# Hybrid decoder layer: x factor loads spread in time, eight weight buffers in the branches, the partial sum added by an accumulating load, residual rows later

## Chip, cores and metric

The kernel runs on one core of a Trainium2 chip. The metric is the device time in microseconds (us) of one execution. The engines are PE (TensorE; PEld is its weight load), DVE (VectorE), ACT (ScalarE), POOL (GpSimd) and SP (SyncE, here only an issuer of DMAs).

## What is computed

One layer for 544 tokens: 512 of a prompt and 8x4 decode tokens. D = 2048, E = 1024. Cut to what matters here:

```
proj = rmsnorm(x) @ w_in                       # 2048 -> 14336: eight parts of 1024, then gpre, 3 x 2048
conv_out = (cb * conv(cc * ch) * silu(cz)) @ w_conv_out            # 1024 -> 2048
ys = gelu(s5(su) * silu(sz))
ssm_out = (ys @ w_glu_a) * sigmoid(ys @ w_glu_b)                   # 1024 -> 2048, twice
attn_out = (attention(aq, memory) * silu(az)) @ w_attn_out         # 1024 -> 2048
g = sigmoid(gpre)
merged = g[0] * conv_out + g[1] * ssm_out + g[2] * attn_out
y = rmsnorm(x + merged @ w_out) * final_norm_g                     # the layer, then the final norm
```

The outputs also hold the new memory keys and values and the new states. All is fp32.

## The kernel before, in words

**Numbers.** Every fp32 operand of a large product is split into a hi part in fp32r (a copy on ACT) and a lo part (source minus hi, on DVE): `split`, L113 to L115. A product is then three matmuls, hi by hi, hi by lo and lo by hi. Weights come from DRAM as raw tiles of 512 KB, loaded by SP, and each is split on the chip. `ws["mark"]` is the lo tile of the latest weight split; `hold` (L135) is a one-element copy on POOL which reads it, so that what POOL issues after it waits for that split.

**Tokens.** T = 544 tokens are two halves of NH = 272; a large matmul is 128x128 by 128x272.

**Stages, in order of time.** First memory keys and values, then projections by `w_in` with `proj` (L149ff, matmuls in L172 to L178), with the convolution, the S5 layer and the attention running beside them as queued pieces (`tick`, `bg`, `later`). One more projection (L1075) opens the silu and gelu of the S5 branch; from there on `w_in` is used by `winograd` (L1083 to L1131): a 2x2 block scheme with seven products in place of eight, n = 1, 5, 6, 3, 7, 2, 4, each 24 matmuls, over x factors XT[n]. XT[1, 2, 3] lie in the x tiles; XT[5], XT[6] and XT[4] are loaded from DRAM (`xf_d`) into tiles of their own, XT[7] over a part of the x tiles that the projection of L1075 still reads. Three `winograd` columns finish the S5 branch's gate, 24 give the sigmoid gates, which go to DRAM (`gt_d`). Beside them `branch_factors` (L1138) writes the seven factors of each branch to DRAM (`fd`).

**Branches, L1188 to L1296.** `winograd2` (L1212 to L1264) is the same scheme for the branch weights: SP loads four raw weight tiles of 512 columns, then seven products of 24 matmuls each follow. For the sums of two weight tiles DVE uses L1243 to L1251. `load_factors` (L1204) loads a branch's 14 factor tiles on POOL into one of two sets, `fsets`. `gate` (L1266) loads two gate tiles, on SP. There are four columns q per weight matrix. Branch 2 (attention) and branch 0 (convolution): the result times the gate goes to `mg_d` in DRAM, first by a plain store, then by a store that adds (L1285). Branch 1: `w_glu_a` times the gate, then `w_glu_b`, sigmoid, product, and an adding store (L1296). The ring of raw weight tiles has 4 + 2 (`bxr`) members.

**Output, L1301 on.** POOL loads the eight tiles of the sum from `mg_d` (L1308), ACT and DVE split them into `mh`, `ml` (L1310). POOL loads the residual rows of x into `yt` (L1323 to L1325). Then eight column blocks jp of `w_out`: a projection, and `residual`, which transposes the result back, adds it to `yt`, squares and scales; the last block also finishes the norm.

**Order.** Each engine works through its own list in order. SP's list holds the weight loads and the gate loads as they are written; a load waits until its buffer is free, and everything behind it on SP waits with it. POOL's list holds factor loads, stores, sum loads and row loads.

Of the kernel before, what the change touches and what calls it, by code (L numbers as in the profile page):

```python
# [20 lines left out]
T = 544  # L21
# [6 lines left out]
def hybrid_step_kernel(  # L28
# [12 lines left out]
    with ctx:  # L41
# [116 lines left out]
        def flush():  # L158
            while later:
                later.pop(0)()  # L160
# [881 lines left out]
        for n in (5, 6, 4):  # L1042
            for hl in range(2):
                P.dma_start(out=XT[n][hl], in_=xf_d[n][hl])
        brs = ExitStack()
# [31 lines left out]
        for hl in range(2):  # L1077
            P.dma_start(out=XT[7][hl], in_=xf_d[7][hl])
# [109 lines left out]
        frs = ExitStack()  # L1188
        fsets = []
        for i in (1, 0):  # L1190
            pool = frs.enter_context(tc.tile_pool(name=f"fset{i}", bufs=1, side="right", reuse_waits="tile"))
            fsets.insert(0, {n: tuple(pool.tile([128, 4, NH], F32R, name=f"b{hl}{n}_{i}") for hl in "hl")
                             for n in (4, 2, 7, 3, 6, 5, 1)})
        mtp = brs.enter_context(tc.tile_pool(name="mgt", bufs=2, reuse_waits="tile"))
# [4 lines left out]
        bxr = bps.enter_context(tc.tile_pool(name="bxr", bufs=2, reuse_waits="tile"))  # L1199
        pbA = bps.enter_context(tc.tile_pool(name="pbA", bufs=2, space=PSUM, reuse_waits="tile"))  # L1200
        pbB = bps.enter_context(tc.tile_pool(name="pbB", bufs=2, space=PSUM, reuse_waits="tile"))
        rings([bxr] * 2, [bxh])
# [9 lines left out]
        def winograd2(w, col0, F, before=None):  # L1212
# [7 lines left out]
            if before:  # L1220
                before()
# [44 lines left out]
        def gate(br, q):  # L1266
            sg = [sgp.tile([128, 2, T], F32, name="sgate") for _ in range(2)]
            for i in range(2):
                nc.sync.dma_start(out=sg[i], in_=gt_d[br, 2 * q + i])
            return sg  # L1270

        def run(g):
            for _ in g:
                pass

        rate[0] = 1
        for br, w, F, nxt in ((2, w_attn_out[0], fsets[0], 1), (0, w_conv_out[0], fsets[1], 2)):
            for q in range(4):
                o = winograd2(w, q * 512, F, (lambda: run(load_factors(F, fd[0], False))) if (br, q) == (2, 0) else None)
                if not q:  # L1280
                    bg.append(load_factors(fsets[nxt % 2], fd[nxt]))
                sg = gate(br, q)
                for i in range(2):
                    V.tensor_mul(o[i], o[i], sg[i])
                    P.dma_start(out=mg_d[2 * q + i], in_=o[i], **({} if br == 2 else {"accum_op": ALU.add}))  # L1285
            tick(1000)
        for q in range(4):
            o = winograd2(w_glu_a[0], q * 512, fsets[0])
            sg = gate(1, q)
# [3 lines left out]
            for i in range(2):  # L1293
                S.activation(o[i], o[i], AF.Sigmoid)
                V.tensor_mul(o[i], o[i], sg[i])
                P.dma_start(out=mg_d[2 * q + i], in_=o[i], accum_op=ALU.add)  # L1296
        bps.close()
        frs.close()
# [4 lines left out]
        mhp = ctx.enter_context(tc.tile_pool(name="mhp", bufs=1, side="right", reuse_waits="tile"))  # L1303
        mh = [mhp.tile([128, T], F32R, name=f"mh{j}") for j in range(16)]
        ml = [mhp.tile([128, T], F32R, name=f"ml{j}") for j in range(16)]
        for i in range(8):
            t = mtp.tile([128, 2, T], F32, name="mgt")
            P.dma_start(out=t, in_=mg_d[i])  # L1308
            for j in range(2):
                split(mh[2 * i + j], ml[2 * i + j], t[:, j])  # L1310
        brs.close()
# [11 lines left out]
        for i in range(5):  # L1323
            hold(yt[i][:, 0:1])
            load_rows(yt[i], i, P)  # L1325
# [41 lines left out]
        for jp in range(7):  # L1367
# [4 lines left out]
            residual(jp, range(5), oT)  # L1372
# [54 lines left out]
```

## Time and profile before

| | |
|---|---|
| median of 3 runs | 2165.47 us (2164.09 to 2172.06) |
| profiled execution, its own time | 2164.23 us |
| span of the profile | 2161.8 us |
| PE busy | 2068.0 us, 96% |
| DVE, ACT, POOL busy | 1284.9, 809.9, 439.5 us |
| mean granted clock of TensorE | 0.984 |
| moved by DMA | 363.59 MB, mean 168 GB/s |
| the chain that ended last | PE 80%, DMA 7%, DVE 5%, POOL 2%, issue 2%, ACT 1% |

The span is that of the trace; the time of the execution is 2.4 us longer. "Busy" counts what an engine computes; for PE a matmul that runs at half clock is busy twice as long, so a high share can hide lost time. "Granted clock" is the share of full speed that TensorE was allowed: 1.00 is 2.4 GHz, 0.50 is 1.2 GHz. In the chain of waits, one follows back from the last instruction what released each step.

### The profile page before, as it was taken

What the parts mean: (1) busy time and instruction counts of PE and PEld (TensorE: products, weight loads), DVE (VectorE), ACT (ScalarE), POOL (GpSimd) and SP (SyncE); (2) the same over time, 40 slices, a digit from 0 to 9 for tenths busy, and PEclk for the clock granted to TensorE, in tenths of its full rate; (3) what the DMA queues carried; (4) which work ended last, traced back from release to release, by engine and by line L of the source; (5) the groups of instructions that cost most, each with busy time, mean ns of one, the idle gap of its engine ahead of it and who ended that gap; (6) DMA issues with size and microseconds to landing.
All of it is one profiled execution on the core that took longest, in us unless ns stands there. A gap on an engine that the chain in (4) does not pass through costs nothing.

```text
span 2161.8 us, 38757 instructions
## 1 busy us (share of the span) xinstructions
PE 2068.0 (96%) x16122; PEld 2016.1 (93%) x16122; DVE 1284.9 (59%) x1877; ACT 809.9 (37%) x1153; POOL 439.5 (20%) x518
## 2 busy tenths in 40 slices
PE   7999999999999999989999999999999899969996
PEld 5899999999999998879999999999899899969996
DVE  6664367943134743238887877767587686753232
ACT  6622222122122433224555555444444344433232
POOL 1008970054201102110121111000121100021121
PEclk9999999999999999999999999999999999989998
DMA  8747612234344626486677776643697955474223
GB/s 261 224 156 143 126 59 90 89 116 108 99 118 146 182 90 224 173 299 172 198 241 221 212 214 207 181 129 110 217 345 252 293 142 164 144 184 137 88 89 83
DMA packets 341619, 363.59 MB, mean 168 GB/s; under 512 B 62507, under 2 KB 288387, under 8 KB 338661
## 3 DMA queue, kind: packets, MB, share of 16 engines
q1 hardware_dynamic: 263712, 211.19, 33.2%
q0 software_dynamic: 38960, 118.48, 17.7%
q10 hardware_dynamic: 38772, 31.46, 5.0%
q8 instruction: 126, 2.06, 0.4%
q14 instruction: 49, 0.39, 0.1%
HBM read 280.82 MB, written 79.73 MB: 167 GB/s over the span
## 4 chain that ended last, share of the span: by engine, by line
PE 80%; DMA 7%; DVE 5%; POOL 2%; issue 2%; ACT 1%; ACTq 1%; DVEq 0%; SPq 0%; POOLq 0%
PE pA L1103 14%; PE pB L1103 11%; PE mmps L172 11%; PE mmps L178 11%; PE mmps L175 11%; PE pbA L1232 5%; PE pbB L1232 4%; DMA raw<-in_w_glu_b_dram 2%; DVE wlo L115 2%; DMA mgt<-mg_d 1%; PE mmps L324 1%; PE mmps L323 1%; PE mmps L325 1%; DMA raw<-in_w_in_dram 1%; DMA bl<-fd 1%
## 5 line engine op out<-in xcount | busy, mean ns | idle before, releaser
L115 DVE TENSOR_TENSOR wlo<-raw,whi 128x1024 fp32r<-128x1024 f32 x395 | 505.9, 1282 | 462.9 <-ACT whi L114 456.0
L114 ACT ACTIVATE whi<-raw 128x1024 fp32r<-128x1024 f32 x395 | 418.5, 1060 | 836.4 <-PE mmps L175 406.0
L172 PE MATMUL mmps<-xh,whi 128*128 128x272 f32 x1856 | 390.3, 291 | 1.5 <-ACT whi L114 1.3
L175 PE MATMUL mmps<-xl,whi 128*128 128x272 f32 x1856 | 389.6, 289 | 0.0
L178 PE MATMUL mmps<-xh,wlo 128*128 128x272 f32 x1856 | 386.7, 289 | 1.1 <-DVE wlo L115 1.1
L175 PEld LDWEIGHTS mmps<-xl,whi 128*128 128x128 f32 x1856 | 293.7, 188 | 4.3 <-issue 4.1
L172 PEld LDWEIGHTS mmps<-xh,whi 128*128 128x128 f32 x1856 | 290.9, 188 | 6.9 <-issue 4.5
L178 PEld LDWEIGHTS mmps<-xh,wlo 128*128 128x128 f32 x1856 | 290.9, 188 | 5.0 <-issue 2.7
L1232 PE MATMUL pbA<-bh,whi 128*128 128x272 f32 x512 | 149.5, 292 | 6.6 <-DVE bo L1256 5.0
L1232 PE MATMUL pbA<-bl,whi 128*128 128x272 f32 x512 | 149.1, 292 | 1.8 <-DMA bl<-fd 1.8
L1232 PE MATMUL pbA<-bh,wlo 128*128 128x272 f32 x512 | 148.9, 292 | 0.0
L1103 PE MATMUL pB<-xh,whi 128*128 128x272 f32 x432 | 126.2, 292 | 3.1 <-ACT whi L114 3.1
L1103 PE MATMUL pB<-xh,wlo 128*128 128x272 f32 x432 | 125.7, 291 | 0.0
L1232 PE MATMUL pbB<-bh,wlo 128*128 128x272 f32 x384 | 113.8, 296 | 12.0 <-DVE wlo L115 12.0
L1103 PE MATMUL pB<-xl,whi 128*128 128x272 f32 x432 | 125.3, 290 | 0.0
L1103 PE MATMUL pA<-xth,whi 128*128 128x272 f32 x432 | 124.4, 288 | 0.7 <-DVE sgate L1124 0.6
L1103 PE MATMUL pA<-xh,wlo 128*128 128x272 f32 x432 | 124.8, 289 | 0.0
L1103 PE MATMUL pA<-xh,whi 128*128 128x272 f32 x432 | 124.7, 289 | 0.0
L1103 PE MATMUL pA<-xth,wlo 128*128 128x272 f32 x432 | 124.6, 288 | 0.0
L1103 PE MATMUL pA<-xl,whi 128*128 128x272 f32 x432 | 124.4, 288 | 0.0
L1103 PE MATMUL pA<-xtl,whi 128*128 128x272 f32 x432 | 124.1, 287 | 0.0
L172 PE MATMUL mmps<-mh,whi 128*128 128x272 f32 x448 | 93.9, 294 | 21.0 <-ACT mh L114 21.0
(402 smaller groups left out, 4595.2 us busy)
## 6 DMA issues: line engine op xcount, KB each, us to landing
raw<-in_w_in_dram SPq DMA_DIRECT2D x224, 512.0 KB, 3.9
fd<-fs POOLq DMA_DIRECT2D x84, 272.0 KB, 4.0
raw<-in_w_out_dram SPq DMA_DIRECT2D x32, 512.0 KB, 3.4
gt_d<-sgate ACTq DMA_DIRECT2D x24, 544.0 KB, 3.1
sgate<-gt_d SPq DMA_DIRECT2D x24, 544.0 KB, 7.1
mg_d<-bo POOLq DMA_DIRECT2D x24, 544.0 KB, 8.4
bh<-fd POOLq DMA_DIRECT2D x21, 544.0 KB, 7.7
bl<-fd POOLq DMA_DIRECT2D x21, 544.0 KB, 9.0
```

The source lines that it names most:

```text
L114: S.activation(hi, src, AF.Copy)
L115: V.tensor_sub(lo, src, hi.bitcast(F32))
L172: nc.tensor.matmul(ps[m][:, n, :NH], lh, rh(kt, n), start=(kt == 0), stop=False)
L175: nc.tensor.matmul(ps[m][:, n, :NH], lh, rl(kt, n), start=False, stop=False)
L178: nc.tensor.matmul(ps[m][:, n, :NH], ll, rh(kt, n), start=False, stop=(kt == nk - 1))
L323: nc.tensor.matmul(o, lh, hi[:, q, :], start=(kt == 0), stop=False)
L324: nc.tensor.matmul(o, lh, lo[:, q, :], start=False, stop=False)
L325: nc.tensor.matmul(o, ll, hi[:, q, :], start=False, stop=(kt == 15))
L1103: nc.tensor.matmul(ps, a[:, k, :], t[:, k, :], start=new and i == 0, stop=i == 23, skip_group_check=not new)
L1232: nc.tensor.matmul(ps[:, s], a[:, k, s * 128:(s + 1) * 128], t[:, k, :], start=new and i == 0, stop=i == 11, skip_group_check=not new)
```

## The change

1. XT[5] and XT[6] are loaded first, XT[7] after the projection of L1075, and XT[4] after XT[7], behind two holds. Before, XT[4] came ahead of XT[7].
2. `bxr` has four members, so eight raw weight tiles are in the ring. The gates are loaded on POOL, ahead of `winograd2`, in place of SP behind its weight loads. The second factor set is loaded ahead of the first `winograd2`.
3. In branch 1 nothing is stored: the product is the target of an accumulating load of `mg_d`, o[i] += mg_d[i], and each tile is split when a later `tick` takes it from `later`. The split parts go to the factor tiles of set 1, which are free by then, and the last two pairs to new tiles `mhx`, `mlx`. The loads of the sum and their tiles are gone.
4. The residual rows are loaded after the first projection by `w_out`, and `residual` of a block runs one projection later.

```diff
-        for n in (5, 6, 4):
+        def load_xt(n):
             for hl in range(2):
                 P.dma_start(out=XT[n][hl], in_=xf_d[n][hl])
+        load_xt(5)
+        load_xt(6)
...
         ws["st"].close()
-        for hl in range(2):
-            P.dma_start(out=XT[7][hl], in_=xf_d[7][hl])
+        load_xt(7)
+        for t in XT[4]:
+            hold(t[:, 0, 0:1])
+        load_xt(4)
...
-        bxr = bps.enter_context(tc.tile_pool(name="bxr", bufs=2, reuse_waits="tile"))
+        bxr = bps.enter_context(tc.tile_pool(name="bxr", bufs=4, reuse_waits="tile"))
...
-        rings([bxr] * 2, [bxh])
+        rings([bxr] * 4, [bxh])
...
             for i in range(2):
-                nc.sync.dma_start(out=sg[i], in_=gt_d[br, 2 * q + i])
+                P.dma_start(out=sg[i], in_=gt_d[br, 2 * q + i])
...
-                o = winograd2(w, q * 512, F, (lambda: run(load_factors(F, fd[0], False))) if (br, q) == (2, 0) else None)
+                if (br, q) == (2, 0):
+                    for _ in load_factors(F, fd[0], False):
+                        pass
+                sg = gate(br, q)
+                o = winograd2(w, q * 512, F)
                 if not q:
                     bg.append(load_factors(fsets[nxt % 2], fd[nxt]))
-                sg = gate(br, q)
...
+        mh, ml = [], []
+        for pair in fsets[1].values():
+            for t in pair:
+                t = t.rearrange("p k t -> p (k t)")
+                mh.append(t[:, :T])
+                ml.append(t[:, T:])
+
+        def merged(t, k0):
+            for j in range(2):
+                split(mh[k0 + j], ml[k0 + j], t[:, j])
+
         for q in range(4):
+            sg = gate(1, q)
             o = winograd2(w_glu_a[0], q * 512, fsets[0])
-            sg = gate(1, q)
...
-                P.dma_start(out=mg_d[2 * q + i], in_=o[i], accum_op=ALU.add)
+                P.dma_start(out=o[i], in_=mg_d[2 * q + i], accum_op=ALU.add)
+                if (q, i) != (3, 1):
+                    later.append(lambda t=o[i], k0=4 * q + 2 * i: merged(t, k0))
+        frs[0].close()
+        mhx = ctx.enter_context(tc.tile_pool(name="mhx", bufs=2, side="right", reuse_waits="tile"))
...
+        flush()
+        merged(o[1], 14)
...
-        for i in range(8):
-            t = mtp.tile([128, 2, T], F32, name="mgt")
-            P.dma_start(out=t, in_=mg_d[i])
-            for j in range(2):
-                split(mh[2 * i + j], ml[2 * i + j], t[:, j])
...
-        for i in range(5):
-            hold(yt[i][:, 0:1])
-            load_rows(yt[i], i, P)
...
-            residual(jp, range(5), oT)
+            if not jp:
+                for i in range(5):
+                    hold(yt[i][:, 0:1])
+                    load_rows(yt[i], i, P)
+            else:
+                residual(jp - 1, range(5), prev)
+            prev = oT
+        residual(6, range(5), prev)
```

Three places show how the lists of the engines move. The first is SP's list at the third column of `w_glu_b` (raw is a weight tile, sgate a gate tile). Before:

```order
L1217 DMA raw_19623<-in_w_glu_b_dram 128x4x256
L1217 DMA raw_19625<-in_w_glu_b_dram 128x4x256
L1269 DMA sgate_19617<-gt_d_80 128x1088
L1217 DMA raw_19627<-in_w_glu_b_dram 128x4x256
L1269 DMA sgate_19618<-gt_d_80 128x1088
L1217 DMA raw_19629<-in_w_glu_b_dram 128x4x256
```

and now:

```order
L1223 DMA raw_19638<-in_w_glu_b_dram 128x4x256
L1223 DMA raw_19640<-in_w_glu_b_dram 128x4x256
L1223 DMA raw_19642<-in_w_glu_b_dram 128x4x256
L1223 DMA raw_19644<-in_w_glu_b_dram 128x4x256
```

The gates have left SP. They stand now on POOL, between the accumulating loads:

```order
L1312 DMA bo_19646<-mg_d4_89 128x1088
L1273 DMA sgate_19865<-gt_d_80 128x1088
L1312 DMA bo_19647<-mg_d5_90 128x1088
L1273 DMA sgate_19866<-gt_d_80 128x1088
L1312 DMA bo_20108<-mg_d6_91 128x1088
L1312 DMA bo_20109<-mg_d7_92 128x1088
```

The last two rows are the accumulating loads of the last column; no load of the sum follows them.

The second place is ACT's list from the last column of `w_glu_b` into the output projection (whi is the hi part of a weight tile; L1294 and L1310 are the sigmoids). Before:

```order
L114 ACTIVATE whi_20442<-raw_20440 128x1024
L1294 ACTIVATE bo_20085<-bo_20085 128x1088
L114 ACTIVATE whi_20496<-raw_20494 128x1024
L1262 COPY bo_20086<-pbA_20088 128x2x272
L114 ACTIVATE mh0_20321<-mgt_20353 128x544
L114 ACTIVATE mh1_20322<-mgt_20353 128x544
L114 ACTIVATE mh2_20323<-mgt_20359 128x544
L114 ACTIVATE mh3_20324<-mgt_20359 128x544
L1294 ACTIVATE bo_20086<-bo_20086 128x1088
L114 ACTIVATE whi_20550<-raw_20548 128x1024
L114 ACTIVATE mh4_20325<-mgt_20365 128x544
```

and now:

```order
L114 ACTIVATE whi_20378<-raw_20376 128x1024
L1310 ACTIVATE bo_20108<-bo_20108 128x1088
L114 ACTIVATE whi_20432<-raw_20430 128x1024
L1266 COPY bo_20109<-pbA_20111 128x2x272
L1310 ACTIVATE bo_20109<-bo_20109 128x1088
L114 ACTIVATE bh1_1_16548<-bo_20108 128x544
L114 ACTIVATE bl1_1_16549<-bo_20108 128x544
L114 ACTIVATE whi_20486<-raw_20484 128x1024
L114 ACTIVATE mhx_20331<-bo_20109 128x544
L114 ACTIVATE mhx_20333<-bo_20109 128x544
L114 ACTIVATE whi_20540<-raw_20538 128x1024
```

Before, sixteen hi copies of the sum stood among the splits of the first weight tiles; now four do, two ahead of the third weight tile's split and two ahead of the fourth's.

The third place is POOL's list at the x factors (xth5 is the hi tile of XT[5]; xl and xh are where XT[7] goes). Now:

```order
L1045 DMA xth5_9898<-xf5_82 128x2176
L1045 DMA xtl5_9899<-xf5_82 128x2176
L1045 DMA xth6_9896<-xf6_83 128x2176
L1045 DMA xtl6_9897<-xf6_83 128x2176
L1045 DMA xl_139<-xf7_84 128x8x272
L1045 DMA xh_138<-xf7_84 128x8x272
L137 COPY xth4_9894<-wlo_10086 128x1
L137 COPY xtl4_9895<-wlo_10086 128x1
L1045 DMA xth4_9894<-xf4_81 128x2176
L1045 DMA xtl4_9895<-xf4_81 128x2176
```

Before, the two loads of xth4 and xtl4 stood directly behind those of xtl6, ahead of xl and xh, and without holds.

## Rows read from the trace of the kernel before

**Rows 1.** The page, part 1: busy time of each engine, share of the span, instructions.
```profile
PE 2068.0 (96%) x16122; PEld 2016.1 (93%) x16122; DVE 1284.9 (59%) x1877; ACT 809.9 (37%) x1153; POOL 439.5 (20%) x518
```

**Rows 2.** Table by stretches of the span: stretch and its length, busy time and (instructions) of PE, PEld, DVE, ACT, POOL, then granted clock, share of DMA engines busy, GB/s.
```profile
955.00:1005.00 50.00, 38.14 (x265) 36.94 (x264) 34.85 (x38) 20.82 (x29) 0.00 (x0) 0.86 0.91 269
1005.00:1543.00 538.00, 536.92 (x4279) 536.14 (x4278) 416.07 (x440) 270.20 (x380) 56.48 (x108) 1.00 0.60 183
1543.00:1575.00 32.00, 27.82 (x200) 26.53 (x199) 19.57 (x20) 10.80 (x13) 7.42 (x14) 0.95 1.00 344
1575.00:1675.00 100.00, 100.00 (x801) 100.00 (x800) 81.36 (x76) 46.09 (x54) 21.35 (x50) 1.00 0.90 296
1675.00:1740.00 65.00, 56.60 (x421) 56.16 (x420) 44.23 (x41) 23.02 (x27) 12.17 (x23) 0.92 0.89 268
1740.00:1905.00 165.00, 156.40 (x1207) 155.32 (x1207) 122.04 (x113) 74.75 (x86) 6.26 (x8) 0.97 0.49 142
1905.00:1965.00 60.00, 38.98 (x285) 37.30 (x283) 23.96 (x28) 19.35 (x28) 12.88 (x26) 0.86 0.87 236
1965.00:2125.00 160.00, 159.80 (x1281) 159.34 (x1281) 46.96 (x63) 50.66 (x111) 31.31 (x35) 1.00 0.23 77
```

**Rows 3.** PE's timeline, four of the instructions before which it stood idle: start, duration, engine, line, operation, tiles, and in brackets the idle time and what ended it.
```profile
970.12 0.59 PE L1103 MATMUL pB<-xth,whi 128*128 128x272 f32 x1 [8.66 <-ACT whi L114]
...
1698.88 0.39 PE L1232 MATMUL pbB<-bh,wlo 128*128 128x272 f32 x1 [4.04 <-DVE wlo L115]
...
1796.15 0.59 PE L1232 MATMUL pbB<-bh,wlo 128*128 128x272 f32 x1 [3.07 <-DVE wlo L115]
...
1942.15 1.28 PE L172 MATMUL mmps<-mh,whi 128*128 128x272 f32 x4 [16.89 <-ACT mh L114]
```

**Rows 4.** Two stretches at half clock, columns as in rows 2.
```profile
965.82:976.06 10.24, 5.50 (x22) 5.19 (x23) 7.81 (x7) 2.50 (x3) 0.00 (x0) 0.50 1.25 334
...
1795.30:1802.10 6.80, 5.95 (x26) 5.95 (x27) 6.77 (x8) 0.79 (x1) 0.00 (x0) 0.50 0.65 229
```

**Rows 5.** Around the x factors: DVE's timeline, then the packets, MB and share of 16 engines' time of two DMA queues in 950 to 962 (q0 is POOL's, q1 SP's), of q1 in 964 to 975, and the DMA issues at 940.5 (XT[6], lo) and 941.5 (XT[4], lo): transfers, KB each, us from issue to landing.
```profile
967.69 1.22 DVE L1109 TENSOR_TENSOR sum<-raw 128x1024 f32<-128x1024 f32 x1 [1.15 <-DMA raw<-in_w_in_dram]
...
q0 software_dynamic: 475, 3.72, 76.4%
...
q1 hardware_dynamic: 472, 0.24, 9.7%
...
q1 hardware_dynamic: 1924, 0.97, 44.3%
...
xtl<-xf POOLq DMA_DIRECT2D x1, 1088.0 KB, 16.8
...
xtl<-xf POOLq DMA_DIRECT2D x1, 1088.0 KB, 23.0
```

**Rows 6.** A step of the glu: SP's list of issues, a link of the chain of waits (start, us, what), and DVE's wait for the sum of two weight tiles.
```profile
1782.14 0.34 SPq L1269 DMA_DIRECT2D sgate<-gt_d  x1
1786.08 0.37 SPq L1217 DMA_DIRECT2D raw<-in_w_glu_b_dram  x1
...
1780.93 12.68 DMA raw<-in_w_glu_b_dram
...
1793.73 1.22 DVE L1243 TENSOR_TENSOR bsum<-raw 128x1024 f32<-128x1024 f32 x1 [7.68 <-DMA raw<-in_w_glu_b_dram]
```

**Rows 7.** The end of a glu step (timelines of ACT, DVE and POOL): a weight split's hi part, the copy of the last product, a split's lo part, the two adding stores. Then the copies of the sum's split, all 14 on record: least, median and greatest duration in ns, first and last start. Then how long the stores into `mg_d` took from issue to landing in 1700 to 1900.
```profile
1777.78 1.06 ACT L114 ACTIVATE whi<-raw 128x1024 fp32r<-128x1024 f32 x1 [0.46 <-PE pbA L1232]
1778.75 0.59 ACT L1262 COPY bo<-pbA 128x544 f32<-128x544 f32 x1
...
1784.83 1.23 DVE L115 TENSOR_TENSOR wlo<-raw,whi 128x1024 fp32r<-128x1024 f32 x1 [1.59 <-ACT whi L114]
...
1780.06 0.85 POOL L1296 DMA_DIRECT2D mg_d<-bo  x1 [40.94 <-DVE bo L1295]
1782.40 0.85 POOL L1296 DMA_DIRECT2D mg_d<-bo  x1 [1.49 <-DVE bo L1295]
...
L114 ACT ACTIVATE mh<-mgt x14: 641/650/660, 1918.0 to 1957.6; 128x544 fp32r<-128x544 f32 x14
L115 DVE TENSOR_TENSOR ml<-mgt,mh x14: 717/720/727, 1918.7 to 1958.4; 128x544 fp32r<-128x544 f32 x14
...
DMA to landing us min/median/max: 5.6/9.1/10.2
```

**Rows 8.** DMA issues in 1914 to 1941: transfers, KB each, median us to landing; and a link of the chain of waits there.
```profile
mg_d<-bo POOLq DMA_DIRECT2D x2, 544.0 KB, 16.6
mgt<-mg_d POOLq DMA_DIRECT2D x2, 544.0 KB, 18.1
raw<-in_w_out_dram SPq DMA_DIRECT2D x2, 512.0 KB, 19.0
...
1922.95 18.48 DMA mgt<-mg_d
```

**Rows 9.** DMA queues in 1675 to 1726, from the conv branch's last column into the first glu column: packets, MB, share of 16 engines' time; and the issues of conv weights.
```profile
q0 software_dynamic: 2306, 8.91, 59.5%
q1 hardware_dynamic: 5264, 6.88, 40.5%
...
raw<-in_w_conv_out_dram SPq DMA_DIRECT2D x2, 512.0 KB, 11.3
```

More of the change, by code (lines that the diff above doesn't have):

```diff
@@ L1184, in hybrid_step_kernel @@
         xs.close()
-        frs = ExitStack()
+        frs = [ExitStack(), ExitStack()]
+        ctx.callback(frs[1].close)
         fsets = []
         for i in (1, 0):
-            pool = frs.enter_context(tc.tile_pool(name=f"fset{i}", bufs=1, side="right", reuse_waits="tile"))
+            pool = frs[i].enter_context(tc.tile_pool(name=f"fset{i}", bufs=1, side="right", reuse_waits="tile"))
             fsets.insert(0, {n: tuple(pool.tile([128, 4, NH], F32R, name=f"b{hl}{n}_{i}") for hl in "hl")
                              for n in (4, 2, 7, 3, 6, 5, 1)})
-        mtp = brs.enter_context(tc.tile_pool(name="mgt", bufs=2, reuse_waits="tile"))
         bps = ExitStack()
@@ L1210, in load_factors, with winograd2 @@
                 yield
-        def winograd2(w, col0, F, before=None):
+        def winograd2(w, col0, F):
             blk = {}
@@ L1219, in winograd2 @@
             a11, a12, a21, a22 = blk[0, 0], blk[0, 1], blk[1, 0], blk[1, 1]
-            if before:
-                before()
             def product(ps, n, src, new):
@@ L1268, in gate @@
             for i in range(2):
-                nc.sync.dma_start(out=sg[i], in_=gt_d[br, 2 * q + i])
+                P.dma_start(out=sg[i], in_=gt_d[br, 2 * q + i])
             return sg
-        def run(g):
-            for _ in g:
-                pass
         rate[0] = 1
@@ L1295, in hybrid_step_kernel @@
                 V.tensor_mul(o[i], o[i], sg[i])
-                P.dma_start(out=mg_d[2 * q + i], in_=o[i], accum_op=ALU.add)
+                P.dma_start(out=o[i], in_=mg_d[2 * q + i], accum_op=ALU.add)
[3 more added lines that the diff above has]
+        mhx = ctx.enter_context(tc.tile_pool(name="mhx", bufs=2, side="right", reuse_waits="tile"))
+        for j in range(2):
+            mh.append(mhx.tile([128, T], F32R, name="mhx"))
+            ml.append(mhx.tile([128, T], F32R, name="mlx"))
+        flush()
+        merged(o[1], 14)
         bps.close()
-        frs.close()
+        brs.close()
         rings()
         open_std()
-        mhp = ctx.enter_context(tc.tile_pool(name="mhp", bufs=1, side="right", reuse_waits="tile"))
-        mh = [mhp.tile([128, T], F32R, name=f"mh{j}") for j in range(16)]
-        ml = [mhp.tile([128, T], F32R, name=f"ml{j}") for j in range(16)]
-        for i in range(8):
-            t = mtp.tile([128, 2, T], F32, name="mgt")
-            P.dma_start(out=t, in_=mg_d[i])
-            for j in range(2):
-                split(mh[2 * i + j], ml[2 * i + j], t[:, j])
-        brs.close()
         ytp = ctx.enter_context(tc.tile_pool(name="ytp", bufs=1, side="right", reuse_waits="tile"))
```

## The prediction, written before the change was run

> **What bounds the kernel now.** I read the busy line first: PE works for 96% of the span [rows 1]. One matmul group of this kernel is 128x272, and where nothing disturbs it PE starts 801 of them in 100 us, 8.0 per us, at a granted clock of 1.00, the upper of the two levels, 2.4 GHz [rows 2] (the stretch from 1575 to 1675). So a stretch with fewer matmuls than eight per us has lost the difference, whether PE stood still or ran at half clock. The table of stretches gives: 955 to 1005, 265 matmuls in 50 us, 16.9 us lost (**A**, the start of the x factors); 1543 to 1575, 200 in 32 us, 7.0 lost (**B**, the start of the branches); 1675 to 1740, 421 in 65 us, 12.4 lost, and 1740 to 1905, 1207 in 165 us, 14.1 lost (**C**, 26.5 in all); 1905 to 1965, 285 in 60 us, 24.4 lost (**D**, the merged sum). The rest of the middle is full: 4279 in 538 us and 1281 in 160 us [rows 2]. The change touches only A to D: 74.8 us, so even with all of it gone the time would be 2089.
>
> Then PE's own timeline says what each wait was for [rows 3]. In A, PE waits 8.66 us for a hi copy of ACT; in C, 4.04, 3.07 and similar waits for the lo part of a weight split; in D, 16.89 us for the hi copy of the merged sum. After a long wait the granted clock is 0.50 (1.2 GHz) for a while [rows 4]: 5.50 us of matmuls from 965.82 at half clock lose 2.75 us more. A wait thus costs more than its length, and counting matmuls takes that in.
>
> **The sum, part by part**, against the profiled execution (2164.2 us, 1.2 under the median of 2165.5).
>
> *A, x factors.* ACT waits for DVE's sum of two weight blocks, which waits for the fourth weight load: it can run only at 967.69 [rows 5]. Why is that load late? While XT[5], XT[6] and XT[4] load, the weights' queue q1 moves 472 packets in 12 us, as many as the factors' q0 (475), 39 per us each; a factor packet is some 8 KB and a weight packet 0.5 KB, so the weights get 0.24 MB against 3.72. Later, beside XT[7], which has small packets, q1 moves 1924 in 11 us, 175 per us. The last transfer of XT[6] lands at 940.5+16.8 = 957.3, that of XT[4] at 941.5+23.0 = 964.5 [rows 5]. The change puts XT[4] behind XT[7], so the slow 7.2 us leave the weights' path. Between 957.3 and 967.7 q1 moved about 7.2x39+3.2x175 = 840 packets; at 175 per us they take 4.8 us, so the sum can run 5.6 us earlier. Of the 8.66 us wait 3.1 stay. With half of the 2.75 us at half clock I take **7.0**. Lower end 0: another wait (the gelu steps on DVE and ACT stand in the same order) takes the place. Upper end 14: all but the 3.1. The holds in front of XT[4] wait for the last weight split of the projection, which is over before PE leaves that projection, so before XT[7] is in; behind them on POOL stand only the branch factors, and XT[4] belongs to the last product.
>
> *B, branch start.* Two gates (1.1 MB) leave SP for a place behind the 14 factor loads on POOL, and two more weight loads (1.05 MB) come into the two new buffers. DMA is full there, at 344 GB/s [rows 2], so 3.2 us of transfers go and 3.0 come: **0**, ends -3 and +2.
>
> *C, branches and glu.* On SP a gate stood ahead of the third and the fourth weight load of each block column, and a gate waits for DVE's product with the gate before it. At 1782.14 SP issues the second gate, and the fourth weight load only at 1786.08 [rows 6]; with a landing of up to 12.68 us the chain then goes through that load, and DVE's sum of two weight blocks stands idle 7.68 us for it. In this stretch the DMA engines are busy 0.49 of the time [rows 2]: the load is late because it is issued late. With eight buffers and no gate on SP, all four loads of the next product can be issued as this one's splits free the buffers, a whole product (24x7/8 = 21 us) ahead, against that landing of 12.68. What comes new: in three of the four glu steps ACT and DVE get four merge splits, ACT 4x0.65 and DVE 4x0.72 = 2.9 us [rows 7]; DVE has 122.04 busy of 165 us [rows 2], 15.5 of each 21, so 18.4 with them. It fits, but not always in the right place: I leave half of it, 1.5 us three times. Gain 26.5-4.5 = **22**; ends 12 (first rival) and 26. POOL's issue is dearer (0.85 us for a transfer of this size [rows 7], SP's 0.34 [rows 6]) but on no path, since the gate is needed 21 us later.
>
> *D, merged sum.* Before, the last accumulating store must land, then the load of the sum, both beside the residual rows (544x2048 fp32, 4.5 MB): medians 16.6 and 18.1 us [rows 8]. Afterwards one accumulating load stands there, and the rows come one projection later. Let X be the end of the last branch product. In the glu steps X is 1778.7 and POOL issues the two transfers at 1780.06 and 1782.40, X+1.4 and X+3.7 [rows 7]. An accumulating load does not occur in the trace; the nearest row is the accumulating store of the same tile, 5.6 at the least, 9.1 median, 9.3 at this place and 10.2 at the most [rows 7]. I take 9.3. So the first tile lands at X+10.7; two hi copies (1.3) and the weight split behind them on ACT and DVE (1.06, 1.23) end at X+14.3. ACT has the splits of the output projection's first two weight blocks ahead of these copies, the third behind them, the fourth behind the second tile's. Two blocks are 96 matmuls, so PE has 12 us of work from X on, and then waits 2.3. The second tile lands at X+13.0 and is through at X+16.6, due at X+20.3: no wait. Gain 24.4-2.3 = **22**; ends 14 (a landing of 16.6 even without the rows: 7.3 more, and some half clock) and 24.
>
> *Residuals.* The residual of one projection runs beside the next; 5 and 6 come together before the last block, with 10 transposed tiles on four banks. DVE is busy 46.96 us in 160 [rows 2], 6.7 per projection, of which four weight splits are 4.9; the rest, 1.8 us, is what one more residual could cost. I take **-1**, ends 0 and -3. The rows' loads, now from about X+18, slow the second projection's weights to some 19 us [rows 8]; its last block is issued near X+17 and due at X+42, so it hides.
>
> Sum: 7+0+22+22-1 = 50; 2164.2-50 = **2114**. All lower ends together give 2144, all upper ones 2098.
>
> **Rivals.**
> *DMA engines, not the issue order, bound the end of the conv branch* (0.20). For: in 1675 to 1726 the shares of the queues are 59.5% and 40.5%, together all of the 16 engines' time, and a conv weight load takes 11.3 us [rows 9]. The same bytes must pass. Against: 1740 to 1905 at 0.49. Then the 12.4 us of 1675 to 1740 stay, but for the part that I leave anyway: 10 less gain, **2124**. The Trainium skill ("DMA: Bandwidth & Descriptors", Issuing engines are not separate DMA queues) says that loads of all issuing engines run on the same 16 DMA engines, so that another issuer saves only the time to issue. By that rule moving the gates to POOL is worth nothing where these are full, which the rows of 1675 to 1726 bear out, and something where SP stands waiting, as at 1782.
>
> *The first stage gains nothing* (0.10): the weights come earlier but the gelu chain on ACT and DVE holds the split. **2121**.
>
> *Accumulating loads land late* (0.12). A gate's load stands between the two, and ACT works in order: behind the merge copies stand the weight splits. The second load must be through by the seventh product, X+18: 18-3.7-1.3-1.06-1.23 = 10.7 us at most; beyond it, every microsecond is lost three times, and in D from 9.3 on. At 13 us (between 10.2 and 16.6) that is 3x2.3+3.7 = 10.6, with one stretch at half clock (5.95 us of matmuls at 1795.3 [rows 4], 3 us) some 14: **2128**.
>
> *Slower, by the same wait* (0.03): the cost is 4L-41.4 for a landing of L. At L = 22.9 it eats the 50 us, from 25.6 on the kernel is slower by over 0.5%; at 27 us it is 67, **2181**. For: 18.48 us was seen for a load of the sum [rows 8]. Against: that one stood beside the residual rows, which leave the place, and in the glu stretch nothing took over 10.2.
>
> *The change does not do what it says* (0.02): the scheduler's rows show the new order, so only a wait that I don't see could keep all of it.
>
> **How the numbers follow.** My forecast has 0.53. The range, **2097 to 2140**, runs from nearly all upper ends to nearly all lower ones and holds the first three rivals; outside stay the slower case, no change, and combinations, together under 0.2. A measurement of this kernel tells 0.5%, 10.8 us, from no change. Faster 0.93 (forecast and three rivals, less a rest), the same 0.04, slower 0.03.
>
> **What would show it.** By stretches, matmuls lost against eight per us: A about 10, B 7, C under 6, D under 4. XT[4] lands behind XT[7]; no half clock in the glu steps; four weight loads of a product issued without a gap; accumulating loads landing in 9 to 10 us and in the tail no wait over 3 us. It is wrong if the chain still shows weight loads of the branches (first rival), a wait for ACT hi copies in the middle of glu_a products (third), or if in A the sum still runs at 967.

## The result, and the profile after

The changed kernel takes 2107.19 us (median of 4, 2105.97 to 2112.99), before 2165.24 (2164.09 to 2172.06). The ratio is 0.9731, 95% interval [0.9704, 0.9758]: 58 us faster. The same kernel run again later gave 0.9730 [0.9715, 0.9744]. Forecast: 2114 in a range of 2097 to 2140.

The table by stretches of the kernel after, columns as in [rows 2]:

```profile
955.00:1005.00 50.00, 44.33 (x331) 43.89 (x331) 39.05 (x44) 23.62 (x33) 0.00 (x0) 0.93 0.96 282
1537.00:1569.00 32.00, 27.08 (x197) 26.02 (x196) 19.79 (x19) 10.86 (x13) 7.96 (x15) 0.95 1.00 344
1669.00:1734.00 65.00, 64.97 (x519) 64.75 (x518) 53.46 (x50) 28.36 (x34) 15.06 (x28) 1.00 1.05 325
1734.00:1885.00 151.00, 150.56 (x1201) 150.16 (x1201) 128.31 (x124) 80.41 (x96) 8.44 (x12) 1.00 0.46 134
1885.00:1910.00 25.00, 25.00 (x202) 25.00 (x201) 9.54 (x10) 9.36 (x12) 8.12 (x17) 1.00 0.83 212
```

Against eight matmuls per us the first row now loses 8.6 us (before 16.9), the second 7.4 (7.0), the next two 1.0 together (26.5) and the last nothing (24.4 in the row of 1905 to 1965). The end of the conv branch runs at full rate with the DMA engines busy all the time.

Matmul counts of fixed windows compare badly where the stages shift, so from here on I cut at the same work in each kernel: **A** from the first matmul over x factors to the first of the branches, **B** the first branch product column, **C** from the second to the last glu matmul, **D** from there to the end of the first projection by `w_out`. Each row below is such a stretch of the kernel after, A to D:

```profile
960.72:1541.48 580.76, 572.68 (x4538) 571.26 (x4537) 452.55 (x480) 292.10 (x412) 59.71 (x114) 0.99 0.64 194
1541.48:1568.53 27.05, 23.54 (x169) 22.67 (x170) 14.84 (x14) 7.86 (x9) 5.31 (x10) 0.94 1.07 373
1568.53:1885.11 316.58, 316.11 (x2521) 315.49 (x2520) 264.56 (x249) 154.70 (x183) 52.70 (x100) 1.00 0.71 222
1885.11:1909.36 24.25, 24.25 (x196) 24.25 (x194) 9.44 (x10) 8.72 (x12) 7.61 (x16) 1.00 0.83 213
```

and of the kernel before:

```profile
958.28:1547.80 589.52, 574.90 (x4539) 572.73 (x4537) 454.11 (x480) 292.70 (x412) 60.72 (x116) 0.99 0.63 189
1547.80:1574.26 26.46, 23.96 (x169) 22.87 (x169) 14.20 (x14) 7.86 (x9) 3.18 (x6) 0.94 1.08 377
1574.26:1916.29 342.03, 325.03 (x2521) 323.51 (x2520) 254.99 (x237) 148.12 (x171) 42.43 (x89) 0.97 0.69 213
1916.29:1965.86 49.57, 28.35 (x200) 26.45 (x198) 17.34 (x22) 15.94 (x24) 10.23 (x18) 0.83 0.91 242
```

The gain is 8.8 in A, -0.6 in B, 25.4 in C, 25.3 in D. Ahead of A the kernel after is 2.4 us later, behind D 0.1 later: 56.4, the difference of the two spans (2161.8 and 2105.4). The 2.4 us are scatter: nothing is changed there, and a run of the old program with a later part changed reaches A at 960.98 too.

What PE still waits for in A (timeline of PE, idle time in brackets; before: 8.66 [rows 3]):

```profile
968.33 0.39 PE L1109 MATMUL pB<-xth,whi 128*128 128x272 f32 x1 [4.43 <-ACT whi L114]
970.08 0.59 PE L1109 MATMUL pB<-xth,wlo 128*128 128x272 f32 x1 [1.24 <-DVE wlo L115]
```

The accumulating loads at a glu step and at the end (POOL's list), and their least, median and greatest time to landing; the stores of [rows 7] had 5.6, 9.1 and 10.2:

```profile
1760.54 0.87 POOL L1312 DMA_DIRECT2D bo<-mg_d  x1 [37.94 <-DVE bo L1311]
1761.10 0.85 POOL L1273 DMA_DIRECT2D sgate<-gt_d  x1
1762.88 0.86 POOL L1312 DMA_DIRECT2D bo<-mg_d  x1 [0.93 <-DVE bo L1311]
...
1885.93 0.87 POOL L1312 DMA_DIRECT2D bo<-mg_d  x1 [36.84 <-DVE bo L1311]
1889.70 0.87 POOL L1312 DMA_DIRECT2D bo<-mg_d  x1 [2.90 <-DVE bo L1311]
...
DMA to landing us min/median/max: 5.7/6.5/10.0
```

### The profile page after: what moved, and what is told of

It reads as the page before. It is cut to its first block, busy times and chain, and to the rows that moved or that the text cites. A ratio compares the mean times of both kernels' runs of the same rounds, so it can differ in the third digit from the quotient of the medians.

```text
span 2105.4 us, 38714 instructions
## 1 busy us (share of the span) xinstructions
PE 2053.1 (98%) x16122; PEld 2004.0 (95%) x16122; DVE 1283.5 (61%) x1877; ACT 809.0 (38%) x1153; POOL 447.2 (21%) x536
## 4 chain that ended last, share of the span: by engine, by line
PE 79%; issue 5%; DMA 5%; DVE 4%; POOL 3%; ACTq 1%; ACT 1%; POOLq 0%; SPq 0%; DVEq 0%
PE mmps L178 12%; PE mmps L172 12%; PE mmps L175 11%; PE pA L1109 11%; PE pB L1109 9%; PE pbA L1236 8%; PE pbB L1236 6%; DVE wlo L115 1%; DMA bl<-fd 1%; PE mmps L324 1%; PE mmps L323 1%; PE mmps L325 1%; PE aux L717 1%; DMA raw<-in_w_in_dram 1%; POOL pw L567 1%
## 5 line engine op out<-in xcount | busy, mean ns | idle before, releaser
L1236 PE MATMUL pbB<-bl,whi 128*128 128x272 f32 x384 | 110.4, 288 | 1.8 <-DMA bl<-fd 1.8
```

The lines of the kernel that those rows point to most:

```text
L1236: nc.tensor.matmul(ps[:, s], a[:, k, s * 128:(s + 1) * 128], t[:, k, :], start=new and i == 0, stop=i == 11, skip_group_check=not new)
```

## The experiments

My theory after the result: A, C and D each lost time to a transfer that came late, by the order in which queues moved it or by the buffer it waited for. Open were: buffers or gates in C; the accumulating load or the residual rows in D; the order of the loads or of the gelu steps in A; and what late accumulating loads cost. All times are medians, all ratios are to the kernel before on the same chip.

| kernel | us | ratio, 95% interval | A | B | C | D |
|---|---|---|---|---|---|---|
| before | 2165.2 | 1 | 589.5 | 26.5 | 342.0 | 49.6 |
| changed | 2107.2 | 0.9731 [0.9704, 0.9758] | 580.8 | 27.0 | 316.6 | 24.3 |
| changed, again | 2108.1 | 0.9730 [0.9715, 0.9744] | 581.4 | 26.6 | 317.8 | 24.3 |
| six buffers | 2136.6 | 0.9876 [0.9843, 0.9910] | 579.6 | 25.7 | 350.1 | 24.2 |
| seven buffers | 2114.1 | 0.9759 [0.9744, 0.9773] | 580.0 | 26.4 | 323.7 | 24.2 |
| gates on SP | 2112.3 | 0.9766 [0.9730, 0.9803] | 578.6 | 28.5 | 322.6 | 24.2 |
| six buffers, gates on SP | 2133.5 | 0.9856 [0.9838, 0.9875] | 579.0 | 26.4 | 343.3 | 24.3 |
| x order as before | 2115.3 | 0.9775 [0.9746, 0.9804] | 589.9 | 27.0 | 316.5 | 24.2 |
| XT[5], XT[6] in small packets | 2110.6 | 0.9755 [0.9724, 0.9787] | 582.6 | 26.8 | 316.8 | 24.2 |
| XT[6] in small packets | 2107.6 | 0.9742 [0.9702, 0.9781] | 580.2 | 26.6 | 317.4 | 24.3 |
| attention output stored early | 2128.6 | 0.9820 [0.9794, 0.9847] | 594.5 | 26.9 | 324.8 | 24.2 |
| store, then load | 2122.4 | 0.9809 [0.9772, 0.9846] | 579.9 | 27.0 | 322.4 | 32.2 |
| rows early | 2117.9 | 0.9780 [0.9751, 0.9810] | 582.8 | 26.5 | 317.4 | 33.3 |
| before, rows late | 2147.9 | 0.9920 [0.9891, 0.9950] | 588.7 | 26.5 | 342.6 | 31.6 |

**Six buffers.**
```diff
-        bxr = bps.enter_context(tc.tile_pool(name="bxr", bufs=4, reuse_waits="tile"))
+        bxr = bps.enter_context(tc.tile_pool(name="bxr", bufs=2, reuse_waits="tile"))
...
-        rings([bxr] * 4, [bxh])
+        rings([bxr] * 2, [bxh])
```


> The changed kernel with six raw weight buffers in the branches in place of eight (bxr 2 for 4); the gates stay on POOL. Measured of the changed kernel: from the start of the second branch product to the last matmul of the glu 316.6 us, before 342.0. If the buffers set when a weight load is issued (in the trace of before, the third and fourth loads are released by the end of a weight split on DVE), that stretch goes back to 336 to 342 us, and the kernel to 2107+20 to 25 = 2127 to 2132. If it was the gates that stood ahead of these loads on SP, as the prediction put it, the stretch stays under 322 us and the kernel under 2113.

C is 350.1: the whole gain of C and 8 us more are gone. The chain of waits in a glu step shows what issues the late load; start, us, what:

```profile
1772.82 1.15 DVE wlo L115
1773.97 0.02 issue
1773.99 11.98 DMA raw<-in_w_glu_b_dram
```

No gate stands on SP here. The load starts when a weight split on DVE has freed its buffer. Five columns lose time: the third and fourth of the convolution branch (30.2 and 27.2 us) and the last three of `w_glu_a` (28.5, 26.7 and 27.2); the others of C take 21.0 to 21.2.

**Gates on SP, in the code behind the weight loads; and with six buffers.**
```diff
-                P.dma_start(out=sg[i], in_=gt_d[br, 2 * q + i])
+                nc.sync.dma_start(out=sg[i], in_=gt_d[br, 2 * q + i])
...
-            sg = gate(1, q)
             o = winograd2(w_glu_a[0], q * 512, fsets[0])
+            sg = gate(1, q)
```


> The changed kernel with the gates back on SP behind the weight loads of the product; eight buffers stay. If the gates on SP made the weight loads late, the stretch from the second branch product to the last glu matmul grows from 316.6 us by 10 us or more and the kernel reaches 2117 or more. If the number of buffers was the cause, a load issued a whole product ahead can stand behind a gate for some us at no cost: stretch under 320, kernel 2105 to 2111.

In the list that the scheduler wrote, a gate stands ahead of the first of four weight loads and another ahead of the second. SP's issues in a glu step:

```profile
1804.40 0.34 SPq L1273 DMA_DIRECT2D sgate<-gt_d  x1
1805.54 0.37 SPq L1223 DMA_DIRECT2D raw<-in_w_glu_a_dram  x1
1806.74 0.34 SPq L1273 DMA_DIRECT2D sgate<-gt_d  x1
1810.69 8.42 SPq L1223 DMA_DIRECT2D raw<-in_w_glu_a_dram  x3
```

C is 322.6, 6.0 us more than with the gates on POOL, between the two bets, and not for the weights: all of it lies in three columns of `w_glu_a` (24.7, 22.8 and 22.9 us against 21.0 to 21.7), and the wait there is for a hi copy on ACT, which stands behind the merge copies that wait for the accumulating load. Accumulating loads (time to landing: least, median, greatest) and one of the three waits of PE:

```profile
DMA to landing us min/median/max: 5.9/9.0/10.6
...
1815.75 0.40 PE L1236 MATMUL pbB<-bh,whi 128*128 128x272 f32 x1 [1.30 <-ACT whi L114]
```

In the glu steps the first load of each pair now takes 9.09, 8.84 and 8.86 us, with the gates behind it on POOL 5.70, 5.91 and 5.70. The gate on SP moves beside the accumulating load; on POOL's queue it comes after it. So with eight buffers this part of the change does pay, but by way of the accumulating loads.

> The changed kernel with six buffers and the gates on SP: the second part undone as a whole, the accumulating load, the x order and the late rows stay. Stretch from the second branch product to the last glu matmul: 342.0 before, 350.1 with six buffers and the gates on POOL, 322.6 with eight and the gates on SP. If buffers and gates add up, 350+6 = 356 us and the kernel 2141; if the gates on SP matter only where they make the accumulating load late, and with six buffers PE waits for weights anyway, 347 to 352 us and the kernel 2134 to 2138.

C is 343.3, next to 342.0 before: with the second part undone, all that the change gains in C is gone. It is also less than with six buffers and the gates on POOL, so the two don't add up. PE waits 1.0 to 1.4 us for ACT in the same three places, and less for weights. DVE's timeline in the first of these glu steps, with the gates on POOL and then on SP:

```profile
1786.10 1.23 DVE L1247 TENSOR_TENSOR bsum<-raw 128x1024 f32<-128x1024 f32 x1 [6.99 <-DMA raw<-in_w_glu_b_dram]
1787.24 0.72 DVE L115 TENSOR_TENSOR bh<-bo,bh 128x544 fp32r<-128x544 f32 x1
...
1789.64 1.22 DVE L115 TENSOR_TENSOR wlo<-raw,whi 128x1024 fp32r<-128x1024 f32 x1
...
1785.48 1.23 DVE L1247 TENSOR_TENSOR bsum<-raw 128x1024 f32<-128x1024 f32 x1 [1.83 <-DMA raw<-in_w_glu_b_dram]
1786.62 1.22 DVE L115 TENSOR_TENSOR wlo<-raw,whi 128x1024 fp32r<-128x1024 f32 x1
```

The sum of two weight blocks of the next column stands in DVE's list ahead of the last splits of this one, which is how a late load holds up a product that doesn't use it. With the gates on POOL two merge splits and another weight operation stand between that sum and the split that PE waits for (3.5 us from start to start), with the gates on SP nothing does (1.1). The three columns of `w_glu_a` are 3.3, 1.3 and 2.2 us shorter with the gates on SP; the rest of the 6.8 us I have not followed.

**Seven buffers** (bufs=3).

> The changed kernel with seven raw weight buffers in place of eight. From the second branch product to the last glu matmul: 316.6 us with eight, 350.1 with six. If the release of a buffer by a weight split sets when a load is issued, only each product's fourth load is late with seven; since that is the tile that the second of the seven products needs (it is the sum of the third and the fourth tile), most of the loss should be there still: 330 to 345 us, kernel 2120 to 2135. If buffers only cover jitter, the loss is small with one missing: under 322, kernel under 2113.

Most of the loss is not there, so the expectation was wrong: C is 323.7. Nearly all of the loss is one column, the third of the convolution branch, 27.8 us, where the DMA engines are full (1669 to 1700: share 1.02). First the link of the chain of waits there, then PE's wait:

```profile
1667.54 20.74 DMA raw<-in_w_conv_out_dram
...
1690.81 0.60 PE L1236 MATMUL pbA<-bh,wlo 128*128 128x272 f32 x1 [4.08 <-DVE wlo L115]
```

The glu columns stay at 21.0 to 22.2. The weight loads of 1780 to 1860 land in 3.3 and 9.6 us (medians of `w_glu_b` and `w_glu_a`), the one of the chain took 20.74. One missing buffer shortens the lead of a load but leaves it longer than a landing, except where landings are long.

**X order as before** (`load_xt` in the order 5, 6, 4, then 7, no holds).

> The changed kernel with the x factors in the old order: XT[4] ahead of XT[7], no holds. From the first matmul of the x products to the first of the branches: 580.8 us in the changed kernel, 589.5 before. If the big packets of XT[4] hold up the weights, it goes back to 588 to 590 and the kernel to 2107+8 = 2115 (2113 to 2117). If other things gave that gain (the order in which the scheduler put the gelu steps), it stays under 584 and the kernel under 2111.

A is back at 589.9 and PE's wait too:

```profile
973.25 0.59 PE L1106 MATMUL pB<-xth,whi 128*128 128x272 f32 x1 [8.98 <-ACT whi L114]
```

But the gelu steps don't stand as in the changed kernel: DVE has its old list again, with the second gelu step ahead of the sum. DVE in the kernel before; ACT and DVE in this run; DVE in the changed kernel, where the sum comes first:

```profile
965.81 0.72 DVE L1070 TENSOR_TENSOR stage<-stage,gate 128x544 f32<-128x544 f32 x1 [3.75 <-ACT gate L1069]
...
968.21 0.66 ACT L1073 ACTIVATE gate<-gate 128x544 f32<-128x544 f32 x1 [4.07 <-DMA od_d<-o_all]
...
968.90 0.72 DVE L1074 TENSOR_TENSOR stage<-stage,gate 128x544 f32<-128x544 f32 x1 [4.00 <-ACT gate L1073]
970.82 1.22 DVE L1112 TENSOR_TENSOR sum<-raw 128x1024 f32<-128x1024 f32 x1 [1.20 <-DMA raw<-in_w_in_dram]
...
965.90 1.22 DVE L1115 TENSOR_TENSOR sum<-raw 128x1024 f32<-128x1024 f32 x1 [2.20 <-DMA raw<-in_w_in_dram]
```

The weights are what the sum waits for last each time. With the old list, though, weights alone that came sooner could have saved only 1.2 us of the 4, since until then DVE stood in the gelu step. That step waited for ACT, and ACT for one of the last stores of the attention output (od_d), which landed 6.4 us after the first x matmul before, 6.7 here and 2.0 in the changed kernel. So with the old order of loads two transfers came later. By an estimate from the rows the second gelu step could have been through at about 965.5 in the changed kernel, even with the old list: ACT is free at 963.75, and an issue of 0.33 us, the step's 0.66 on ACT and its 0.72 on DVE follow. That is just ahead of the weights. But this run takes back loads and list together and does not tell them apart.

**Small packets.** The tiles of XT[5] and XT[6], then of XT[6] alone, get padding, so that their rows are no longer one piece.
```diff
-            XT[n] = tuple(xtp.tile([128, 8, NH], F32R, name=f"xt{hl}{n}") for hl in "hl")
+            XT[n] = tuple(xtp.tile([128, 8, NH + (4 if n in PAD else 0)], F32R, name=f"xt{hl}{n}")[:, :, :NH]
+                          for hl in "hl")
```


> The changed kernel with the tiles of XT[5] and XT[6] padded by four columns per block, so that their loads move in packets of 1088 bytes, as those of XT[7], and not of 8704. Measured before the edit: beside the big packets the weights' queue gets about 39 packets per us, beside small ones 100 to 200. If queues share packet by packet, the weights' queue moves over 90 packets per us from 952 us on (changed kernel: 36), DVE's sum for the second product starts 4 us or more earlier and the wait of 4.43 us for it goes; but the factors themselves come later (4096 small packets at 100 to 200 per us: done about 965), so XT[6] can be waited for. Net forecast: 3 us faster, 2104 (2100 to 2110). If the share goes by bytes, nothing moves for the weights and the kernel stays at 2107 or gets slower.

The queues in 954 to 958 (packets, MB, share of 16 engines' time) of the changed kernel:

```profile
q0 software_dynamic: 156, 1.22, 77.9%
q10 hardware_dynamic: 154, 0.30, 19.2%
q1 hardware_dynamic: 153, 0.08, 9.6%
```

and with small packets, in the same window:

```profile
q0 software_dynamic: 715, 0.77, 68.9%
q1 hardware_dynamic: 635, 0.33, 40.7%
```

Packet for packet, as expected: the weights get four times the bytes, the factors 0.77 MB where they got 1.22. PE's wait falls from 4.43 to 2.14 us:

```profile
966.89 0.59 PE L1111 MATMUL pB<-xth,whi 128*128 128x272 f32 x1 [2.14 <-ACT whi L114]
...
981.90 0.36 PE L1111 MATMUL pA<-xh,whi 128*128 128x272 f32 x1 [1.80 <-DMA xh<-xf]
```

but a new one, for XT[7], comes up, and the stretch at half clock stays at 6.83 us. The time is not lower; the share by packets is shown, a gain is not.

> The changed kernel with only XT[6] padded, so that XT[5] (ahead of the weights) moves in large packets and XT[6] in packets of 1088 bytes. With both padded, the weights' queue moved 117 to 205 packets per us from 954 us on, PE's wait for the second product fell from 4.4 to 2.1 us, but XT[7] came late (1.8 us). Here the factors should all be in 3 us earlier than there: stretch from the first x matmul to the first branch matmul 577 to 580 us (580.8 in the changed kernel), kernel 2104 (2101 to 2108). If the late XT[7] decides, 582 and 2109.

A is 580.2, as in the changed kernel: no gain, no late XT[7] either. The wait for the second product is 2.14 us here too, but the half-clock stretch after it is again 6.82 us long, and a wait for a weight split comes up later:

```profile
997.12 0.39 PE L1111 MATMUL pA<-xth,wlo 128*128 128x272 f32 x1 [1.58 <-DVE wlo L115]
```

**Attention output stored early.**
```diff
                     P.tensor_mul(o_all[:, ct, 0:TP], o_all[:, ct, 0:TP], gz[:, 0:TP])
+                    P.dma_start(out=od_d[ct * 128:(ct + 1) * 128, 0:TP], in_=o_all[:, ct, 0:TP])
...
-        for ct in range(8):
-            S.dma_start(out=od_d[ct * 128:(ct + 1) * 128, :], in_=o_all[:, ct, :])
+        S.dma_start(out=od_d.rearrange("(k p) t -> p k t", p=128)[:, :, TP:T], in_=o_all[:, :, TP:T])
```


> The changed kernel, and the attention output is stored to DRAM in pieces: each block's 512 prompt columns on POOL as soon as they are gated, in the projections before, and only the 32 decode columns at the end in one small store on ACT. Before, eight stores of 272 KB on ACT's queue ran beside the loads of XT[5] and XT[6] and the weights: three queues took turns, 64 to 200 packets each in 2 us. If the queues take turns packet by packet, one queue less makes the big factor packets end 2 to 3 us earlier and the weights after them go at 200 per us at once: PE's wait for the second product falls from 4.4 to under 2.5 us, the stretch from the first x matmul to the first branch matmul from 580.8 to 575 to 578, the kernel from 2107 to 2103 (2101 to 2106). If the DMA engines' bytes decide, the last stores only move and the wait stays at 4.

A failure that tells nothing of its question: the scheduler put four other weight loads, issued from 948.1 to 960.6, ahead of the one that the sum for the second product needs (965.6, landing 16.84 us later), and PE waits for that:

```profile
984.88 0.59 PE L1109 MATMUL pB<-xth,whi 128*128 128x272 f32 x1 [17.77 <-ACT whi L114]
```

C is 8.2 us longer too; nearly all of it is the fourth column of the convolution branch (29.4 us), where PE waits 5.67 us for a weight split. I did not follow that.

**Store, then load, in place of the accumulating load.**
```diff
-                P.dma_start(out=o[i], in_=mg_d[2 * q + i], accum_op=ALU.add)
+                P.dma_start(out=mg_d[2 * q + i], in_=o[i], accum_op=ALU.add)
+            for i in range(2):
+                P.dma_start(out=o[i], in_=mg_d[2 * q + i])
```


> The changed kernel with an accumulating store to DRAM and then a plain load of the sum back into the same tiles, in place of the one accumulating load; all else as changed, the residual rows late. This makes the merged tiles land late on purpose. X is the start of the copy of the last product of w_glu_b. From the run with the gates on SP: with the first accumulating load at 9.1 us instead of 5.7, a glu step took 22.8 to 24.7 us and not 21.0 to 21.7, so the first tile may land 7.2 us after its issue at the latest. Here it lands about X+1.4+8 (store) +5.5 (load) = X+15, 6.4 us past that. If ACT's order is what passes the delay on, as the third rival has it: 6.4 and 1.7 of half clock, three times, 24 us in the stretch from the second branch product on, and about 12 us more in the first output projection (24.3 now), so 2107+36 = 2143 (2130 to 2155). By the prediction's own formula 4L-41.4 with L = 15.8 for the second tile it would be 22 us, 2129. If late tiles don't hold up PE, under 2112.

15 us slower, where I expected 36. The tiles land late as planned (about X+17 and X+21 in the first step), but the scheduler moved the merge copies on ACT behind the last split of the column that runs beside them. They now hold up the first splits of the column after it: those of `w_glu_b` take 23.7, 23.8 and 22.8 us where they took 21.0, 21.0 and 21.2, which is the 5.8 us that C loses. As a price list for late landings in the changed kernel's order the run fails; the run with the gates on SP, where the order is the changed kernel's, serves better. In D the loss is 8.0 us, for the most part a wait for the second merged tile. The first adding store of each of the three steps, with the gate behind it on POOL, took 5.63, 5.83 and 5.59 us, like the accumulating load in the same place in the changed kernel (5.70, 5.91 and 5.70). One of the waits in C, and the one in D:

```profile
1787.02 0.39 PE L1236 MATMUL pbA<-bh,wlo 128*128 128x272 f32 x1 [1.36 <-DVE wlo L115]
...
1916.16 0.82 PE L172 MATMUL mmps<-mhx,whi 128*128 128x272 f32 x2 [6.07 <-ACT mhx L114]
```

**Rows early; rows late alone.** The edits are the fourth part of the change, taken back in the changed kernel and made alone in the one before.

> The changed kernel with the residual rows loaded early again, ahead of the output projection, and residual in step with its own projection; the accumulating load stays. Measured: from the last glu matmul to the end of the first output projection 49.6 us before, 24.25 in the changed kernel (24.1 is the projection without a wait). If the accumulating load alone removes the wait, 24.3 to 27 us and the kernel within 3 us of 2107. If the rows' traffic beside it matters as much (sum loads took 18 us beside them before), the last accumulating loads land in 14 us or more, the projection takes 31 to 38 us and the kernel 2114 to 2122.

> The kernel before with the fourth part alone: residual rows after the first output projection, residual one projection later; accumulating stores and loads of the sum stay. From the last glu matmul to the end of the first output projection: 49.6 us before. If the rows' traffic made most of that wait, 30 to 36 us and the kernel 13 to 19 us faster than before; if the chain of store, load and split behind two buffers makes it, 40 us or more and the kernel under 10 us faster.

With the accumulating load and early rows D is 33.3, with store and load and late rows 31.6, with both 24.3, with neither 49.6. DMA issues in 1888 to 1895 of the run with early rows:

```profile
yt<-in_x_prompt_dram POOLq DMA_DIRECT2D x4, 512.0 KB, 18.9
bo<-mg_d POOLq DMA_DIRECT2D x2, 544.0 KB, 18.5
```

Row loads stand ahead of both accumulating loads in POOL's list there. Each part alone takes 16 to 18 of the 25.3 us; together they take all of it, so they overlap by 9.

**The control.**

> The changed kernel as it is, on the same chip beside the others, as their base: 2107 (2105 to 2110), stretches within 1.5 us of the first profile: 580.8 from the first x matmul to the first branch matmul, 316.6 from the second branch product to the last glu matmul, 24.25 from there to the end of the first output projection.

It came out so, 2108.1. No experiment is clearly faster than the changed kernel.

## Why the prediction was right, point by point

**Sum.** 50 forecast, 57 measured on the profiled executions (2164.2 and 2107.2): the signs and places were right, and A, C and D gave 1.8, 3.4 and 3.3 us more than I took.

**A, 7.0 forecast, 8.8 measured.** That the large packets of XT[4] held up the weights holds: the gain goes with the x order, and small packets halve PE's wait. But the forecast took the weights to be all that the sum waited for, and the gelu steps to keep their place. Before, DVE was in the second gelu step until 966.53 and the sum then waited only 1.15 us for weights [rows 5]; 5.6 us, or 4, were not to be had from earlier weights alone. The same change made the store land earlier that this step waited for, and the scheduler put the step behind the sum. The forecast had neither, so that its 7.0 came near is in part luck. DVE's sum starts 5.2 us after the first x matmul, before 9.4: 4.2 us earlier, not 5.6, and 4.4 us of wait stay where I left 3.1. In return the shorter wait halves the stretch at half clock (6.83 us at 0.50, before 10.24 [rows 4] and a second of 3.41) and the three later waits of about 1 us are gone, more than the 1.4 I had put down for it.

**B, 0 forecast, -0.6 measured.** Two profiles of the changed kernel give 27.0 and 26.6; as forecast.

**C, 22 forecast, 25.4 measured; one step had the wrong cause.** The forecast said that a gate ahead of the third and fourth load made them late [rows 6]. The runs show the buffers: with eight and the gates on SP no column of C waits for a weight load; with six and the gates on POOL five do, all of them columns that lost time before. The rows could have told it: the third load starts at 1780.93 in the chain, right at the end of a weight split, and 1786.08 is the end of the next one (1784.83 and 1.23 in [rows 7]). An issue that follows a gate in the list needn't wait for it. The 1.5 us left for merge splits in each of three steps were too much: these columns take 21.0 to 21.9 us in the two profiles of the changed kernel.

**D, 22 forecast, 25.3 measured.** The term mis-sized is the landing: 9.3 us taken from the accumulating stores; the last two accumulating loads took 5.87 and 7.05. An accumulating load is not cheaper than an adding store; the stores of [rows 7] had a gate load beside them on SP's queue (the first of each pair took 8.41, 8.44 and 8.47 us in the glu steps), and in the last column there is none. Landing at X+6.6 or so, the first is through before PE has done its two blocks, and PE waits for nothing. That the landing depends on what stands ahead of it or moves beside it is shown by the runs with early rows (16.1 and 20.8 us) and with the gates on SP.

**Residuals, -1 forecast.** Behind D the kernel is 0.1 us later: no more than scatter.

**The rivals.** *DMA full at the end of the conv branch*: shown wrong. DMA is busy all of 1669 to 1734 and PE loses nothing; short were the leads of the loads, not the engines. By the Trainium skill's rule ("DMA: Bandwidth & Descriptors", Issuing engines are not separate DMA queues) the gates' move to POOL should save no more than time to issue, and for the weights the runs agree. The 6.0 us that it does save come from the order within POOL's queue, which that rule doesn't speak of. *The first stage gains nothing*: did not happen, but the gelu step was as near to holding the sum as said under A. *Late accumulating loads*: did not happen, but my limit was wrong. I counted the second load's (10.7 us). The first has a tighter one: ACT's merge copies of the first tile stand ahead of the split of product 2, and PE's list has two matmuls of product 2 ahead of product 7, so that split is due three us sooner than I had it. From the run with the gates on SP, where 8.84 to 9.09 us cost PE waits of 1.3 to 1.6, the limit is about 7.5. With the 9.3 that I had forecast this rival would have come in part; what kept it out is that the first load took 5.7, with the gate behind it and not beside it. The forecast had no reason to expect that: here it was right by luck. The formula 4L-41.4, on which the slower rival rests, stays untested, since late tiles made the scheduler write another order.

## What to carry to other kernels

When a load is issued late, look at what ended right before the issue: here the end of a split, to 0.1 us, named the buffer and not the neighbour in the list. Count the lead that a ring of buffers gives against the longest landing of the stretch; seven of eight were enough where landings took 3 to 10 us and not where one took 21. Put a transfer that is not urgent on the queue of the urgent one, behind it, rather than on a queue of its own beside it; here that was worth 6.0 us with eight buffers. Keep large packets off the time in which small ones are waited for. And when an edit makes the scheduler write another list, compare the lists before you put the gain down to the edit alone.

## What the runs showed of the hardware

In the stretches read here, queues that had work all the time moved packet for packet, whatever the size: 156, 154 and 153 packets in 4 us on three queues with 7.8, 1.9 and 0.5 KB each. An accumulating load of 544 KB landed in 5.7 us where the gate load came behind it on the same queue, in 9 beside a gate load on another queue, in 16 to 21 behind the row loads. An adding store of the same tile took as long: 5.6 with the gate behind it, 8.4 with the gate beside it.
